# Self-attention values projected with the activations stationary and the weights moving

## The chip, the cores and the metric

The kernel runs on one core of a Trainium2 chip. The metric is the device time of one execution in microseconds. A core has TensorE (matmuls; PE in the profile, with PEld for its loading of the stationary operand), VectorE (DVE), ScalarE (ACT), GpSimd (POOL) and SyncE (SP), which here issues all the DMA transfers. Matmul results go to PSUM, and the other engines bring them to SBUF.

## The reference, cut to what matters

One inference step of a 2-layer encoder with 256 prompt tokens and 32 decode tokens, width 1024, all in fp32. Each layer has self-attention over 16 heads of 64, cross-attention into 256 memory tokens and a SwiGLU network. In layer 0, eight heads are chunked attention (A) and eight are stick-breaking attention (B); in layer 1 all sixteen are forgetting attention (C).

```python
def proj_ab(h, w_in):
    ...
    parts = jnp.split(h @ w_in, cuts, axis=-1)      # q, k, v of A; q, k, v of B

def proj_c(h, w_in, b_f):
    z = h @ w_in
    q, k, v = z[..., :w], z[..., w:2 * w], z[..., 2 * w:3 * w]     # then 16 forget gates
...
p = softmax(q @ k * 64 ** -0.5 + bias);  o = p @ v
```

`h` is the RMS-normalised input. The new keys and values of all tokens are outputs as well. The cut lines above are shortened; the reference reshapes to heads of 64 in between.

## The kernel before, in words

**Layout.** Activations are kept transposed: 8 tiles of 128 features by 288 tokens (256 prompt, then 32 decode). A projection (`project`, L151) takes a unit of weights, 128 output features by 1024 inputs, 512 KB. `unit` (L132) loads it into a staging tile `st` (four of them); ScalarE rounds it to fp32r (`hi`, five tiles, L141), VectorE takes the rest (`lo`, four tiles, L142). The activations are split likewise into `hh` and `hl` when a block of x is ready (`Next.block`, L257; `split_scaled`, L241). `mm3` (L145) makes three fp32r matmuls a block, hi by hh, hi by hl and lo by hh, with the weights stationary and 288 tokens moving: 24 matmuls for a unit. The norm's factor is not applied to h; it multiplies the result when PSUM is evacuated, since the sums of squares are ready only later (`Next.scale`, L270; `cur.then` holds evacuations back until the factor `cur.r` is there).

**Pairs of heads.** A unit is a pair of heads, so layer 0 has 24 units (`mix_ab`, L763) and layer 1 has 24 and one for the gates (`mix_c`, L870). `pairs` (L803) goes over eight pairs: project q, k and v of a pair (`evac_q` L716, `evac_kv` L721), start its attention, and insert some steps of the cross-attention's memory projections. Attentions are generators: each project calls `tick` (L176), which lets every attention that is under way make its next step, so that softmax on the other engines runs under the next projection.

**The values.** v comes out as features by tokens, and the product with the probabilities needs tokens on partitions. `v_natural` (L328) therefore transposes v on TensorE in three pieces (L330 to L332, tile `vt`) and ScalarE copies them to `vn` (L334, L335). `prompt_pv` (L380) and `sample_pv` (L407) use it as the stationary and the moving operand.

**Order.** The tile framework orders the instructions of each engine ahead of the run, by the order of the program and its own estimates; each engine then goes through its list in order. SyncE's list holds weight loads, cache and bias loads and the stores, so that a load that waits for a staging tile holds what stands behind it. At the start the first unit (`first`, L74) is loaded in three parts between the parts of x; `rel_lines` (L731) builds a skewed copy of layer 0's bias in DRAM with eight transfers (`skew`), from which every pair of A loads its bias. Layer 1 opens with `begin` (L162): six of eight blocks of two projections, which run while the last blocks of h and the norm's factor are made.

**Pools.** 74 token tiles of 128x288 (`tk`), five `vn` tiles of 384, four PSUM banks for projections (`pj`) and four for attention (`at`). `hidden` (L665) places the 44 tiles of the SwiGLU's hidden layer in `tk`, `w`, `ca` and `w2`; `room` (L584) lends `vn` and `bi` to the cross-attention.

Of the kernel before, what the change touches and what calls it, by code (L numbers as in the profile page):

```python
# [15 lines left out]
P = 128  # L16
# [10 lines left out]
def encoder_step(ctx: ExitStack, tc: tile.TileContext, a):  # L27
# [9 lines left out]
    tk = ctx.enter_context(tc.tile_pool(name="tk", bufs=74))  # L37
# [36 lines left out]
    first = wp.tile([P, 1024], F32, tag="st", bufs=4, name="first")  # L74

    def first_part(c0, c1):
        DMA.dma_start(first[:, c0:c1], a["w_ab"][0][:, c0:c1])

    first_part(0, 256)
    for i in range(4):  # L80
        DMA.dma_start(xh[i], a["xT"][:, 2 * i * NT:2 * (i + 1) * NT])
        if i == 0:
            DMA.dma_start(gain, a["gains"])
            first_part(256, 512)
        if i == 1:
            first_part(512, 1024)
# [45 lines left out]
    def unit(src, st=None, pieces=1):  # L132

        if st is None:
            st = wp.tile([P, 1024], F32, tag="st", bufs=4, name=name("st"))
            DMA.dma_start(st, src)
        hi = wp.tile([P, 1024], F32R, tag="hi", bufs=5, name=name("hi"))
        lo = wp.tile([P, 1024], F32R, tag="lo", bufs=4, name=name("lo"))
        for c in range(pieces):
            b = slice(c * 1024 // pieces, (c + 1) * 1024 // pieces)  # L140
            S.copy(hi[:, b], st[:, b])  # L141
            V.tensor_tensor(lo[:, b], st[:, b], hi[:, b].bitcast(F32), ALU.subtract)  # L142
        return hi, lo
# [107 lines left out]
    class Next:  # L251


        def __init__(self, gi):
            self.gi, self.norm, self.h, self.waiting = gi, Norm(hurry=gi == 8), ([], []), []

        def block(self, m, start=False):  # L257
            g = gain[:, self.gi * KT + m:self.gi * KT + m + 1]
            if self.gi < 8:
                hi, lo = split_scaled(x[m], g, act=True)  # L260
                self.h[0].append(hi)
                self.h[1].append(lo)
            else:
                t = tok("xg")
                V.tensor_scalar(t, x[m], g, None, op0=ALU.mult)
                self.h[0].append(t)
            if not start:
                self.norm.add(x[m])

        def scale(self):  # L270

            if self.gi != 1:
                yield 1
            y = self.norm.columns()
# [53 lines left out]
    def v_natural(v):  # L328
        p = att("vt")
        T.transpose(p[:, 0:128], v[:, 0:128], ident)  # L330
        T.transpose(p[:, 128:256], v[:, 128:256], ident)
        T.transpose(p[0:NS, 256:384], v[:, 256:288], ident)  # L332
        vn = wk.tile([P, 384], F32, tag="vn", bufs=5, name=name("vn"))
        S.copy(vn[:, 0:256], p[:, 0:256])  # L334
        S.copy(vn[0:NS, 256:384], p[0:NS, 256:384])  # L335
        return vn
# [20 lines left out]
    def attend_prompt(q, k, v, vns, j, bias, oh, ol):  # L357

        vn = vns[j] = v_natural(v)
        e = []  # L360
        for hd in range(2):
            r = slice(64 * hd, 64 * hd + 64)
            s = att("sc")
            mm(s[:, 0:128], q[r, 0:128], k[r, 0:128])
            mm(s[:, 128:384], q[r, 128:256], k[r, 0:256])
            e.append(work("e"))
            softmax(s, QT, bias[hd], e[hd])
        yield 1
        w = []
        for hd in range(2):  # L370
            t = att("tp")
            T.transpose(t[:, 0:128], e[hd][:, 0:128], ident)
            T.transpose(t[:, 128:256], e[hd][:, 128:256], ident)
            T.transpose(t[:, 256:384], e[hd][:, 256:384], ident)
            w.append(work("pt"))
            S.copy(w[hd][:, 0:384], t[:, 0:384])
        yield 1
        prompt_pv(w, vn, oh, ol)

    def prompt_pv(w, vn, oh, ol):  # L380
        po = att("po")
        for hd in range(2):
            r = slice(64 * hd, 64 * hd + 64)
            mm(po[r, 0:256], vn[:, 64 * hd:64 * hd + 64], w[hd][:, 0:256], True, False)
            mm(po[r, 128:256], vn[:, 128 + 64 * hd:192 + 64 * hd], w[hd][:, 256:384], False, True)
# [21 lines left out]
    def sample_pv(w, at, vns, cv, o):  # L407
# [8 lines left out]
        for h in range(4):  # L416
            j, hd = h // 2, h % 2
            c, n = at(j, hd)
            mm(po[32 * h:32 * h + 32, 0:64], w[0:NS, n:n + 32], vns[j][0:NS, 256 + 64 * hd:320 + 64 * hd], False, True)
# [39 lines left out]
    def stick_prompt(q, k, v, vns, j, oh, ol):  # L459
        vn = vns[j] = v_natural(v)  # L460
# [112 lines left out]
    def cross(layer, cur, memory, nxt):  # L573
# [10 lines left out]
        def room(s, i):  # L584

            if i < 10:
                return wk.tile([P, NP], F32R, tag=("vn", "bi")[i % 2], bufs=5, name=name(s))
# [77 lines left out]
    def hidden(s, i):  # L665

        if i < 26:
            return tok(s, F32R)
        i -= 26
        if i < 8:  # L670
            return wk.tile([P, NT], F32R, tag="w", name=name(s))
        if i < 12:
            return wk.tile([P, NT], F32R, tag="ca", bufs=4, name=name(s))
        if i % 2 == 0:
# [46 lines left out]
    def evac_kv(cur, p, dst):  # L721
# [41 lines left out]
    def mix_ab(cur, nxt, memory, w0):  # L763
        o = ([tok("oh", F32R) for _ in range(KT)], [tok("ol", F32R) for _ in range(KT)])
        qs, ks, vs, vns = {}, {}, {}, {}
        w = a["w_ab"]

        def proj(j):
            b = 12 * (j // 4) + j % 4
            kv = 8 * (j // 4) + j % 4  # L770
            qs[j] = evac_q(cur, project(w[b], cur.h, w=w0 if j == 0 else None))
            if j == 0:
                proj.line = rel_lines()
            ks[j] = evac_kv(cur, project(w[b + 4], cur.h), a["kv0"][kv])
            vs[j] = evac_kv(cur, project(w[b + 8], cur.h), a["kv0"][kv + 4])

        def attend(j):
            args = (qs[j], ks[j], vs[j], vns, j)
# [14 lines left out]
        pairs(proj, attend, sample, memory, (0, 0, 0, 0, 2, 2, 2, 8))  # L793
# [9 lines left out]
    def pairs(proj, attend, sample, memory, steps):  # L803
        for j in range(8):
            proj(j)
# [64 lines left out]
    def mix_c(cur, nxt, memory, w0):  # L870
# [11 lines left out]
        qs, ks, vs, vns = {}, {}, {}, {}  # L882

        def proj(j):
            qs[j] = evac_q(cur, project(w[j], cur.h, begun=begun[1] if j == 0 else None))
            ks[j] = evac_kv(cur, project(w[8 + j], cur.h), a["kv1"][j])
            vs[j] = evac_kv(cur, project(w[16 + j], cur.h), a["kv1"][8 + j])

        def attend(j):
# [13 lines left out]
            return attend_prompt(qs[j], ks[j], vs[j], vns, j, bias, o[0][j], o[1][j])  # L903
# [20 lines left out]
        pairs(proj, attend, sample, memory, (3, 1, 1, 1, 1, 1, 1, 5))  # L924
# [4 lines left out]
    w0 = None  # L929
# [27 lines left out]
    "yT": (8, 128, 288), "kv0": (16, 128, 288), "kv1": (16, 128, 288), "lf": (288, 16),  # L957
# [4 lines left out]
def _pack(inputs):  # L962
# [17 lines left out]
    def vals(c):  # L980
# [5 lines left out]
    w_c = np.pad(g["w_in_c"][0], ((0, 0), (0, 112)))  # L986
# [5 lines left out]
        "w_ab": units(g["w_in_ab"][0]), "w_oab": units(g["w_out_ab"][0]),  # L992
# [41 lines left out]
```

## Time and profile before

| | |
|---|---|
| median of 3 runs | 981.52 us (979.58 to 983.31) |
| the profiled execution | 981.77 us |
| its span | 979.9 us |
| TensorE busy, instructions | 960.9 us (98%), 7449 |
| VectorE, ScalarE, GpSimd busy | 60%, 49%, 20% |
| DMA | 163.59 MB, 167 GB/s over the span |
| mean granted clock of TensorE | 0.993 |

In the profile's rows a matmul's duration runs to its modelled end, so consecutive ones overlap; how fast they pass is seen from their starts, or from the count in a window. `128*128 128x288` is a stationary operand of 128 rows by 128 columns and a moving one of 128 partitions by 288 columns. `a<-b,c` is the tile written and the tiles read, the moving operand first. A plain fp32 matmul leaves two records, an fp32r matmul or a transpose one. In the chain of waits a line has the start, the length and what it was; in a timeline, start, length, engine, line, operation and count.

### The profile page before, as it was taken

To read this page: it belongs to the slowest core of one execution; us is meant where nothing else is said; L and a number is where in the kernel's file an instruction comes from. 1 tells how busy PE (TensorE), PEld (TensorE's weight loads), DVE (VectorE), ACT (ScalarE), POOL (GpSimd) and SP (SyncE) were. 2 spreads that over 40 slices of the span, in tenths; PEclk is the share of its full clock that TensorE was granted. 3 is DMA by queue.
4 is the path that set the end of the run, shared out by engine and by line. 5 is a ranking of instruction groups with operands and counts; after the bars stand their busy time and mean duration, and the time that the engine had idled before them with its cause. 6 is when DMAs were issued, how large, how long until landed. Compare 5 with 4: busy or idle time off the path is not lost.

```text
span 979.9 us, 19034 instructions
## 1 busy us (share of the span) xinstructions
PE 960.9 (98%) x7449; PEld 925.1 (94%) x7449; DVE 589.5 (60%) x1135; ACT 483.8 (49%) x854; POOL 194.6 (20%) x293
## 2 busy tenths in 40 slices
PE   8999999999999999999999999999999999999995
PEld 7789999998899999999998999999989999999995
DVE  6686454677676555764565666657757655555452
ACT  5556767555455444444444545445546544444330
POOL 3121001210113222411003234213002222222010
PEclk9999999999999999999999999999999999999997
DMA  7775345544254454455455555545425444444431
GB/s 235 247 248 192 127 165 174 169 168 143 91 179 158 165 173 167 178 193 173 166 201 167 179 191 182 170 160 194 149 100 168 155 159 165 173 164 166 165 109 49
DMA packets 60137, 163.59 MB, mean 167 GB/s; under 512 B 8160, under 2 KB 21520, under 8 KB 60048
## 3 DMA queue, kind: packets, MB, share of 16 engines
q1 hardware_dynamic: 60048, 162.38, 49.0%
q8 instruction: 59, 0.97, 0.4%
q14 instruction: 30, 0.25, 0.1%
HBM read 152.20 MB, written 11.72 MB: 167 GB/s over the span
## 4 chain that ended last, share of the span: by engine, by line
PE 90%; DMA 3%; DVE 3%; issue 1%; ACT 1%; SPq 0%; POOL 0%; DVEq 0%; ACTq 0%; POOLq 0%
PE pj L68 50%; PE dn L68 14%; PE op L68 11%; PE mv L68 5%; DMA st<-w_ab 2%; PE zb L68 1%; PE xs L68 1%; PE xo L68 1%; PE po L68 1%; DVE lo L142 1%; DMA skew<-lined 1%; PE sc L68 1%; PE nr L68 1%; ACT hi L141 1%; PE zs L68 1%
## 5 line engine op out<-in xcount | busy, mean ns | idle before, releaser
L141 ACT CAST hi<-st 128x1024 fp32r<-128x1024 f32 x260 | 272.2, 1049 | 339.4 <-issue 146.9
L68 PE MATMUL pj<-hh,hi 128*128 128x288 f32 (+1 forms) x1352 | 405.1, 300 | 0.0
L68 PE MATMUL pj<-hl,hi 128*128 128x288 f32 (+1 forms) x1352 | 399.8, 296 | 1.7 <-DVE hl L248 1.7
L142 DVE TENSOR_TENSOR lo<-st,hi 128x1024 fp32r<-128x1024 f32 x260 | 323.3, 1244 | 128.8 <-PE dn L68 41.3
L68 PE MATMUL pj<-hh,lo 128*128 128x288 f32 (+1 forms) x1352 | 399.4, 295 | 0.0
L68 PEld LDWEIGHTS pj<-hh,hi 128*128 128x128 f32 x1352 | 256.6, 190 | 6.2 <-issue 4.7
L68 PEld LDWEIGHTS pj<-hl,hi 128*128 128x128 f32 x1352 | 256.5, 190 | 3.3 <-DVE hl L248 3.2
L68 PEld LDWEIGHTS pj<-hh,lo 128*128 128x128 f32 x1352 | 256.7, 190 | 0.0
L68 PE MATMUL dn<-fh,hi 128*128 128x288 f32 x400 | 108.7, 295 | 0.0
L68 PE MATMUL dn<-fh,lo 128*128 128x288 f32 x352 | 103.7, 295 | 0.0
L68 PE MATMUL dn<-fl,hi 128*128 128x288 f32 x304 | 89.5, 294 | 0.0
L68 PE MATMUL op<-ol,hi 128*128 128x288 f32 x256 | 75.5, 296 | 0.0
L68 PE MATMUL op<-oh,lo 128*128 128x288 f32 x256 | 75.5, 295 | 0.0
L68 PE MATMUL op<-oh,hi 128*128 128x288 f32 x256 | 75.1, 296 | 0.0
L68 PEld LDWEIGHTS dn<-fh,hi 128*128 128x128 f32 x400 | 72.5, 188 | 0.0
L68 PEld LDWEIGHTS dn<-fh,lo 128*128 128x128 f32 x352 | 66.1, 188 | 0.0
L213 POOL TENSOR_TENSOR ssq<-ssq,sq 128x288 f32<-128x288 f32 (+1 forms) x37 | 37.0, 1000 | 120.0 <-ACT sq L202 77.8
L68 PEld LDWEIGHTS dn<-fl,hi 128*128 128x128 f32 x304 | 57.1, 188 | 0.0
L691 POOL TENSOR_TENSOR fl<-us,fh 128x288 fp32r<-128x288 f32 x38 | 32.8, 863 | 119.0 <-ACT fh L690 119.0
L686 DVE TENSOR_TENSOR us<-pj,rstd 128x288 f32<-128x288 f32 x44 | 20.1, 457 | 59.4 <-PE pj L68 59.4
L687 POOL TENSOR_TENSOR gs<-gs,sg 128x288 f32<-128x288 f32 x44 | 38.8, 882 | 75.5 <-ACT sg L685 75.5
L68 PEld LDWEIGHTS op<-ol,hi 128*128 128x128 f32 x256 | 48.2, 188 | 0.8 <-issue 0.8
(253 smaller groups left out, 1213.7 us busy)
## 6 DMA issues: line engine op xcount, KB each, us to landing
st<-w_gate SPq DMA_DIRECT2D x44, 512.0 KB, 3.3
st<-w_up SPq DMA_DIRECT2D x44, 512.0 KB, 3.2
st<-w_down SPq DMA_DIRECT2D x44, 512.0 KB, 3.3
st<-w_c SPq DMA_DIRECT2D x25, 512.0 KB, 3.3
st<-w_ab SPq DMA_DIRECT2D x23, 512.0 KB, 4.2
st<-w_xk SPq DMA_DIRECT2D x16, 512.0 KB, 3.6
st<-w_xv SPq DMA_DIRECT2D x16, 512.0 KB, 3.5
st<-w_xq SPq DMA_DIRECT2D x16, 512.0 KB, 4.3
```

The lines of the kernel that those rows point to most:

```text
L68: T.matmul(out, lhsT, rhs, start=start, stop=stop, skip_group_check=True)
L141: S.copy(hi[:, b], st[:, b])
L142: V.tensor_tensor(lo[:, b], st[:, b], hi[:, b].bitcast(F32), ALU.subtract)
L213: eng.tensor_tensor(s[:, :self.n], self.acc[i][:, :self.n], q[:, :self.n], ALU.add)
L686: V.tensor_tensor(us, pu[:, :NT], cur.r, ALU.mult)
L687: G.tensor_tensor(gs, gs, sg, ALU.mult)
L691: G.tensor_tensor(lo, us, hi.bitcast(F32), ALU.subtract)
```

## The change

All values of four pairs (512 columns of weights) are projected at once, by `project_values`, with h as the stationary operand (128 features by 128 tokens) and the weights moving (512 columns). The result has tokens on partitions, so `v_natural` is gone. A group has four units of 1024 columns, each holding two blocks of input features by 512. For the 256 prompt tokens a unit makes 2 blocks x 3 split products x 2 halves = 12 matmuls into two PSUM banks. For the 32 decode tokens it makes 2 x 4 matmuls in plain fp32, from `hs` (unsplit h of the decode tokens) and the unsplit weights in `st`, each with 32 stationary and 128 moving columns, one for each quarter of the output partitions, into a third bank. Evacuation multiplies by the norm's factor per token (a column, `cur.y`), on ScalarE for one half of the prompt and VectorE for the other and for the decode tokens.

Group 0 of layer 0 becomes the first work of the kernel, with its four units loaded between the parts of x; `rel_lines` is placed ahead of it. Group 1 comes ahead of pair 2. In layer 1 group 0 comes ahead of the gates' projection, and `begin` is no longer used there. The `k` outputs remain features by tokens; the value outputs are now tokens by features. Fewer token tiles (69), six `vn` tiles of 512, and `hidden` takes four of them. The host code that packs weights and unpacks outputs follows suit.

```diff
-    tk = ctx.enter_context(tc.tile_pool(name="tk", bufs=74))
+    tk = ctx.enter_context(tc.tile_pool(name="tk", bufs=69))
...
-    first = wp.tile([P, 1024], F32, tag="st", bufs=4, name="first")
-
-    def first_part(c0, c1):
-        DMA.dma_start(first[:, c0:c1], a["w_ab"][0][:, c0:c1])
-
-    first_part(0, 256)
+    first = [wp.tile([P, 1024], F32, tag="st", bufs=4, name=f"first{i}") for i in range(4)]
+
+    def first_part(i, c0, c1):
+        DMA.dma_start(first[i][:, c0:c1], a["w_v"][0, i][:, c0:c1])
+
+    first_part(0, 0, 512)
     for i in range(4):
         DMA.dma_start(xh[i], a["xT"][:, 2 * i * NT:2 * (i + 1) * NT])
         if i == 0:
             DMA.dma_start(gain, a["gains"])
-            first_part(256, 512)
-        if i == 1:
-            first_part(512, 1024)
+            first_part(0, 512, 1024)
+        else:
+            first_part(i, 0, 1024)
...
-        return hi, lo
+        return hi, lo, st
...
+            if gi < 2:
+                self.hs = wk.tile([P, KT * NS], F32, tag="hs", bufs=1, name=name("hs"))
...
+                if self.gi < 2:
+                    V.tensor_scalar(self.hs[:, NS * m:NS * m + NS], x[m][:, NP:NT], g, None, op0=ALU.mult)
...
-    def v_natural(v):
-        p = att("vt")
-        T.transpose(p[:, 0:128], v[:, 0:128], ident)
...
+    def project_values(src, cur, outs, vns, group, w0=None):
+
+
+        h = cur.h
+        p, p_s = [acc("vp") for _ in range(2)], acc("vps")
+        for u in range(4):
+            w = w0[u] if w0 else unit(src[u])
+            with tc.issue_after(warmed.ins):
+                for kk in range(2):
+                    k, c = 2 * u + kk, 512 * kk
+                    for part, wt in ((0, 0), (1, 0), (0, 1)):
+                        for t in range(2):
+                            mm(p[t], h[part][k][:, 128 * t:128 * t + 128], w[wt][:, c:c + 512], k == 0 and part + wt == 0,
+                               k == KT - 1 and wt == 1)
+                for kk in range(2):
+                    k, c = 2 * u + kk, 512 * kk
+                    for j in range(4):
+                        mm(p_s[32 * j:32 * j + 32, 0:128], cur.hs[:, 32 * k:32 * k + 32], w[2][:, c + 128 * j:c + 128 * j + 128],
+                           k == 0, k == KT - 1)
+            if u > 0 or group > 0:
+                tick()
+        vt = [wk.tile([P, 512], F32, tag="vn", bufs=6, name=name("vn")) for _ in range(3)]
+
+        def go():
+            y = cur.y
+            S.activation(vt[0], p[0], AF.Copy, scale=y[:, 0:1])
+            V.tensor_scalar(vt[1], p[1], y[:, 2:3], None, op0=ALU.mult)
+            for j in range(4):
+                r = slice(32 * j, 32 * j + 32)
+                V.tensor_scalar(vt[2][0:NS, 128 * j:128 * j + 128], p_s[r, 0:128], y[96:128, 4:5], None, op0=ALU.mult)
+            for t in range(2):
+                DMA.dma_start(outs[0][group, t], vt[t])
+            DMA.dma_start(outs[1][group], vt[2][0:NS])
+
+        cur.then(go)
...
-            mm(po[r, 0:256], vn[:, 64 * hd:64 * hd + 64], w[hd][:, 0:256], True, False)
+            mm(po[r, 0:256], vn[0][:, 64 * hd:64 * hd + 64], w[hd][:, 0:256], True, False)
...
-        if i < 26:
+        if i < 22:
             return tok(s, F32R)
...
         active.append(cur.scale())
-        pairs(proj, attend, sample, memory, (0, 0, 0, 0, 2, 2, 2, 8))
+        proj.line = rel_lines()
+        values(0)
+        pairs(values, proj, attend, sample, memory, (0, 0, 0, 1, 2, 2, 2, 7))
...
-    def pairs(proj, attend, sample, memory, steps):
+    def pairs(values, proj, attend, sample, memory, steps):
         for j in range(8):
+            if j == 2:
+                values(1)
             proj(j)
...
-        begun = begin([w[24], w[0]], cur.h)
...
         active.append(cur.scale())
-        p = project(w[24], cur.h, begun=begun[0])
+        values(0)
+        p = project(w[16], cur.h)
...
         cur.block(m, start=True)
-        if m == 1:
-            w0 = unit(None, first, 4)
+        if m % 2 == 1:
+            w0.append(unit(None, first[m // 2], 2))
```

More of the change, by code (lines that the diff above doesn't have):

```diff
@@ L273, in scale @@
                 yield 1
-            y = self.norm.columns()
+            y = self.y = self.norm.columns()
             yield 1
@@ L326, in split_o @@
         V.tensor_tensor(ol, p, oh.bitcast(F32), ALU.subtract)
-    def v_natural(v):
-        p = att("vt")
[L330 to L336, printed above, removed]
+    def project_values(src, cur, outs, vns, group, w0=None):
[29 more added lines that the diff above has]
+        cur.then(go)
+        for j in range(4):
+            vns[4 * group + j] = [t[:, 128 * j:128 * j + 128] for t in vt]
     def softmax(s, cols, bias, out):
@@ L991, in _pack @@
         "gains": gains.reshape(9, 8, 128).transpose(2, 0, 1).reshape(128, 72),
[L992 removed]
+        "w_ab": units(w_ab[:, :, 0:2].reshape(1024, 2048)),
+        "w_v": w_v.reshape(4, 4, 2, 128, 512).transpose(0, 1, 3, 2, 4).reshape(4, 4, 128, 1024),
+        "w_oab": units(g["w_out_ab"][0]),
         "w_c": units(w_c), "w_oc": units(g["w_out_c"][0]),
```

68 lines of the change are left out of this document (37 added, 31 removed), and 2 rows, old and new, of the table _OUTS.

## The prediction

> **What bounds the kernel now.** I read the page first, then busy time by stage, then the timeline of TensorE and the chain of waits where the change lies.
>
> ```profile
> span 979.9 us, 19034 instructions
> PE 960.9 (98%) x7449; PEld 925.1 (94%) x7449; DVE 589.5 (60%) x1135; ACT 483.8 (49%) x854; POOL 194.6 (20%) x293
> PE 90%; DMA 3%; DVE 3%; issue 1%; ACT 1%; SPq 0%; POOL 0%; DVEq 0%; ACTq 0%; POOLq 0%
> ```
>
> TensorE carries 90% of the chain that ended last. Busy time says little about its pace, since the records overlap; counts in the windows do. Columns: length, then busy time and number of instructions of each engine, granted clock, DMA share, GB/s.
>
> ```profile
> core 0: us, PE busy (x) PEld busy (x) DVE busy (x) ACT busy (x) POOL busy (x), PEclk, DMA share, GB/s
> ...
> 27.19:60.00 32.81, 30.60 (x255) 26.63 (x254) 23.01 (x71) 17.72 (x46) 4.91 (x15) 1.00 0.76 245
> 60.00:177.50 117.50, 116.93 (x959) 108.73 (x959) 68.39 (x139) 80.53 (x142) 13.28 (x15) 1.00 0.53 174
> ...
> 293.00:422.86 129.86, 129.86 (x987) 129.86 (x986) 81.17 (x121) 61.21 (x86) 41.12 (x43) 1.00 0.49 169
> ...
> 503.00:531.00 28.00, 25.51 (x186) 23.43 (x185) 16.47 (x44) 15.63 (x29) 5.18 (x11) 0.94 0.48 163
> ```
>
> From 293 to 423 us almost all of the 987 matmuls have 288 columns: 129.86/987 = 0.1316 us each, a stream without holes. So in steady state a microsecond comes off the kernel only if TensorE issues a microsecond less. There are holes at two places: the first 60 us, where the DMA share is 0.76, and 503 to 531 us (186 instructions in 28 us).
>
> **What leaves TensorE, per group of four pairs.** Each pair loses its value projection, 24 x 0.1316 = 3.16 us, and three transposes:
>
> ```profile
> 523.47 0.29 PE L68 MATMUL pj<-hh,lo 128*128 128x288 f32 x1
> 523.60 0.27 PE L330 MATMUL vt<-ident,kv 128*128 128x128 f32 x1
> 523.71 0.27 PE L331 MATMUL vt<-ident,kv 128*128 128x128 f32 x1
> 523.82 0.27 PE L332 MATMUL vt<-ident,kv 128*32 128x128 f32 x1
> 524.02 0.93 PE L68 MATMUL sc<-kv,q 64*128 64x128 f32 x8
> ...
> 36.91 0.29 PE L68 MATMUL pj<-hl,hi 128*128 128x288 f32 x1
> 37.04 0.29 PE L68 MATMUL pj<-hh,lo 128*128 128x288 f32 x1
> 37.27 0.88 PE L68 MATMUL po<-pt,vn 128*64 128x256 f32 x8
> ```
>
> The transposes take 524.02-523.60 = 0.42 us. But going from full-array matmuls to matmuls on part of the array costs extra: 37.27-37.04 = 0.23 against 0.13, 0.10 us more. The third transpose bears that now, and the projection before the scores will bear it then, so 0.32 us leaves. Per group: 4 x (3.16+0.32) = 13.9 us.
>
> **What comes: 48 matmuls with 512 moving columns.** No row has 512. The widest of this type has 384:
>
> ```profile
> 97.42 0.34 PE L68 MATMUL zb<-sh,ntrir 128*128 128x384 f32 x1
> 97.60 0.34 PE L68 MATMUL zb<-sl,ntrir 128*128 128x384 f32 x1
> 97.78 0.38 PE L68 MATMUL zb<-ab,nones 128*128 128x128 f32 x2
> ...
> 16.56 0.44 PE L68 MATMUL pj<-hh,hi 128*128 128x288 f32 x1
> 16.80 0.44 PE L68 MATMUL pj<-hl,hi 128*128 128x288 f32 x1
> 17.04 0.37 PE L68 MATMUL pj<-hh,lo 128*128 128x288 f32 x1
> 17.25 0.29 PE L68 MATMUL pj<-hh,hi 128*128 128x288 f32 x1
> 17.38 0.29 PE L68 MATMUL pj<-hl,hi 128*128 128x288 f32 x1
> ```
>
> 384 columns: (97.78-97.42)/2 = 0.18 us, 0.469 ns a column; 288: 0.457 ns. Upper end 0.240 us for 512. Lower end: before 17.04 us matmuls of 288 start 0.24 us apart, 0.833 ns a column; were the later pace exactly twice that, 512 would take 0.213. I take 0.234 (0.457 ns a column, which the 384 confirms): 48 x 0.234 = 11.2 us, between 10.2 and 11.5.
>
> Here a rule disagrees with the row. The Trainium skill, "TensorE: Matmul & The Clock Gate", section "Back-to-back issue gap", gives N/2.4 + 2.5 ns for a warm isolated matmul: 216 ns at 512, and 122.5 ns at 288, where the trace has 131.6. By the rule the 48 would be an estimated 10.4 us. I go by the rows; the rule's outcome is a rival.
>
> **And 32 narrow matmuls for the 32 decode tokens**, plain fp32, 32 columns of the array by 128 moving, each four on the four strips of the array. The nearest rows are the sample scores (four strips, 128 moving, half the rows) and the sample's value product (four strips, 64 moving, all rows); each matmul gives two records.
>
> ```profile
> 42.64 0.44 PE L68 MATMUL ss<-ca,q 64*32 64x128 f32 x8
> 42.88 0.26 PE L68 MATMUL ss<-kv,q 64*32 64x32 f32 x8
> ...
> 53.16 0.32 PE L68 MATMUL os<-ca,pts 128*32 128x64 f32 x8
> 53.41 0.31 PE L68 MATMUL os<-vn,pts 32*32 32x64 f32 x8
> 53.65 0.40 PE L68 MATMUL pj<-hh,hi 128*128 128x288 f32 x1
> ```
>
> Eight records of 128 columns pass in 0.24 us, where a single 128-column transpose takes 0.11: four run side by side, in two turns of 0.12. The full-row case does the same (eight of 64 in 0.25, the switch included). A weight unit has eight such matmuls, so four turns, 0.48 us, and a switch of about 0.10 in and out: 0.68. Per group 4 x 0.68 = 2.7 us. Were the strips to run one after another: 16 x 0.12 + 0.2 = 2.1 per unit, 8.5 per group.
>
> **Sum on TensorE:** 11.2 + 2.7 = 13.9 against 13.9. The wide matmul gains 12.6-11.2 = 1.4 us over the old projections, the dropped transposes 1.3, and the decode tokens eat both. Per group 0 (from -1.0 to +0.3 with the strips parallel), over four groups 0 (-4 to +1).
>
> **Other engines.** One row each:
>
> ```profile
> L142 DVE TENSOR_TENSOR lo<-st,hi 128x1024 fp32r<-128x1024 f32 x260 | 323.3, 1244 | 128.8 <-PE dn L68 41.3
> ...
> L334 ACT COPY vn<-vt 128x256 f32<-128x256 f32 x16 | 5.9, 367 | 0.1
> L335 ACT COPY vn<-vt 32x128 f32<-32x128 f32 x16 | 4.0, 250 | 0.0
> L725 DVE TENSOR_TENSOR kv<-pj,rstd 128x288 f32<-128x288 f32 x32 | 14.3, 450 | 15.7 <-PE pj L68 15.7
> ```
>
> The weight splits stay, 4 a group. ScalarE loses 4 x 0.62 us a group and gains one 512-wide evacuation; VectorE trades 4 x 0.45 for one 512-wide and four small ones, and gets eight small products for the decode tokens per layer. VectorE at 60% and ScalarE at 49% lie under TensorE's stream; were the cover gone it would be about 2 us a group. Four stores a group become three. Nothing on the path.
>
> **Staging.** The narrow matmuls read the unsplit weights, so a value unit's staging tile comes free when TensorE ends the unit, not when VectorE has made lo. Look-ahead falls to three units of 11.2/4 + 0.68 = 3.5 us, 10.4 us. A refill takes 5.0 us landing at its slowest in the start (row below), 1.05 for hi (the ACT hi row there), 1.24 for lo: 7.3. It fits unless SyncE's queue, where stores, bias and cache loads stand behind the waiting weight load, holds it over 3 us. Cost 0 to 2 us a group; I take 0 and count the first group below.
>
> Token tiles fall from 74 to 69. A norm square already waited on one; later blocks of the next norm in the output projection will wait for attention outputs to be read, inside the last 3.2 us pass. 0 to 3 us; I take 0.
>
> **The start.** Here the order changes most: 13.9 us of matmuls on four units come first, fed two x blocks and one weight unit at a time.
>
> ```profile
> 0.00:5.00 5.00, 3.43 (x32) 3.33 (x32) 0.42 (x1) 2.37 (x5) 3.57 (x23) 1.00 0.48 135
> 5.00:10.00 5.00, 4.38 (x14) 3.10 (x13) 4.41 (x6) 3.49 (x10) 4.08 (x7) 1.00 0.97 340
> ...
> 5.11:27.19 22.08, 18.85 (x96) 16.85 (x96) 1.19 (x3) 1.00 0.80 262
> ...
> 11.59 0.61 PE L68 MATMUL pj<-hl,hi 128*128 128x288 f32 x1 [1.09 <-DVE hl L248]
> ...
> 15.55 7.39 DMA skew<-lined
> ...
> 23.37 5.00 DMA st<-w_ab
> 28.45 1.06 ACT hi L141
> ```
>
> Bytes: 0.67 MB by 5 us, then 0.34 MB/us. The four unit-and-x steps need 0.84, 1.66, 2.48, 3.30 MB: 5.5, 7.9, 10.3, 12.8 us. The first matmul comes 0.13 MB later than at 5.11, so 5.6. From there each pair of splits feeds six wide matmuls, not three narrow ones, so I expect no wait like the 1.09 us before 11.59. In the old trace the slow pace ends at 17.04, 5.4 us after matmuls run unbroken (the granted clock reads 1.00 on both sides, the spacing shows it); so in the new one near 11.0. A slow unit lasts 12 x 0.427 + 1.1 = 6.2 us, a fast one 3.5: the first ends at 11.5, the others at 15.0, 18.5, 22.0; with the norm's matmuls (18.83 to 20.09, and 0.6) about 23.9. Then q of pair 0: 27.1.
>
> Old at 27.19: 96 projection matmuls, four projections, 12.6 us of work. New at 27.1: 13.9 + 3.2 = 17.1 us. Lead 4.4 us. With the slow pace to 17.04 as before it is 1.3.
>
> Does it last? From 27.19 to 60 us 255 instructions ran where the next stage's rate (959/117.5) gives 268: 1.6 us of holes, and the chain of waits there runs through the eight skew transfers and weight loads behind them. The skew now lies under the value matmuls, which helps; but the same loads are wanted 4 us sooner. I give back 1.5 (0 to 4.4). Start: -2.9 (-4.4 to +0).
>
> **Layer 1's entry.** The opening of two projections on six of eight blocks goes; the value units cover the norm instead (36 matmuls before block 6 is needed). The gate's chain to the first bias keeps its cover of one projection and three memory steps. 0, bounds -3 to +2.
>
> **Sum.** The profiled execution took 981.77 us (span 979.9 and 1.9 around it). 981.77 + 0 - 2.9 = 978.9; the median of the runs is 0.25 lower, so 978.6.
>
> **Rivals.**
> 1. *512 columns stream at 0.213 us.* Speaks for it: at 17.04 us the pace nearly doubles, and 0.213 is the exact double. Against: 288 and 384 both lie 10% or more above it. 48 x 0.021 x 4 = 4.0 us: 974.6. The Trainium skill's rule quoted above would give nearly the same.
> 2. *The lead is eaten.* The first 60 us wait on transfers, so TensorE arrives sooner and waits longer, on staging tiles held by the narrow matmuls or behind skew in SyncE's queue. Against: 3.3 MB are now asked for in one unbroken run. 981.5, no change.
> 3. *Slower: the strips don't run side by side with 128 rows and 128 columns.* Two at a time: eight turns, 1.16 a unit, +1.9 a group, +7.7: 986.3, and 989.2 without the lead. One at a time: +5.8 a group, +23: 1002. It decides from about 0.9 us a unit, where it cancels the lead. For it: no row has all 128 rows with 128 columns. Against: both neighbours overlap fourfold.
>
> **How the numbers follow.** I call 0.5%, 4.9 us, what a measurement can tell from no change, so faster is below 976.6 and slower above 986.4. Forecast 978.6: 0.52, of which 0.13 falls below 976.6 (lead kept whole, fewer holes). Rival 1: 0.16. Rival 2: 0.20. Rival 3: 0.12, all but 0.02 above 986.4; with unknown stalls taken from rival 2, slower 0.13. Faster 0.29, same 0.58. The range 972.5 to 985 holds rivals 1 and 2 with the bounds of start and tiles, and leaves out rival 3.
>
> **What would show it.** The new wide matmuls 0.234 us apart (0.213: rival 1); eight narrow ones of a unit in about 0.68 us, switches included (over 0.9: rival 3); the slow pace ending near 11 us; the first query projection beginning near 24 us; the stage up to 60 us with no more holes than now. The forecast is wrong if TensorE's count of instructions per microsecond drops in the attention stages, or if weight loads enter the chain in them.

## The result and the profile after

The changed kernel takes 990.73 us (median of 5 runs, 987.13 to 992.12) against 981.52 us before: a ratio of 1.0089, with a 95% interval of 1.0064 to 1.0113. It is 9.2 us slower, where 978.6 was forecast and 985 was the upper end. The profiled execution took 992.12 us, the longest of the five; the one of before took 981.77. What the profiles show below is therefore a loss of 10.4 us, about a microsecond more than the medians.

The page of the profile after: the span, the engines' busy time, the shares of the chain that ended last.

```profile
span 990.4 us, 19040 instructions
...
PE 964.0 (97%) x7465; PEld 913.4 (92%) x7465; DVE 598.7 (60%) x1156; ACT 480.2 (48%) x827; POOL 196.2 (20%) x293
...
PE 87%; DMA 5%; DVE 4%; issue 2%; ACT 1%; POOL 1%; SPq 0%; DVEq 0%; POOLq 0%; ACTq 0%
```

TensorE has 16 more instructions and VectorE is 9 us busier, but none is near its limit except TensorE, and TensorE's share of the chain falls from 90% to 87%, and DMA's rises from 3% to 5%. So something is waited for. Three places in the timeline of TensorE cut the kernel into stages: the first matmul of layer 0's output projection (`op`), the first of layer 1, and the first of layer 1's output projection. Before:

```profile
177.34 0.30 PE L68 MATMUL op<-oh,hi 128*128 128x288 f32 x1
...
492.56 0.29 PE L68 MATMUL pj<-hh,hi 128*128 128x288 f32 x1
...
650.80 0.30 PE L68 MATMUL op<-oh,hi 128*128 128x288 f32 x1
```

and after:

```profile
181.26 0.29 PE L68 MATMUL op<-oh,hi 128*128 128x288 f32 x1
...
496.38 0.39 PE L68 MATMUL vp<-hi,hh 128*128 128x512 f32 x1
...
661.88 0.30 PE L68 MATMUL op<-oh,hi 128*128 128x288 f32 x1
```

| stage | before | after | difference |
|---|---|---|---|
| start and layer 0's self-attention | 177.34 | 181.26 | +3.9 |
| rest of layer 0 | 315.22 | 315.12 | -0.1 |
| layer 1's self-attention | 158.24 | 165.50 | +7.3 |
| from there to the span's end | 329.1 | 328.5 | -0.6 |

The loss lies in the two stages that the change touches. The windows of after show what it is made of (columns as in the prediction: length; busy time and instructions of PE, PEld, DVE, ACT, POOL; granted clock; DMA share; GB/s):

```profile
27.00:60.00 33.00, 30.10 (x210) 25.26 (x208) 16.44 (x49) 14.08 (x33) 2.39 (x16) 0.90 0.68 220
...
531.00:565.00 34.00, 30.28 (x209) 25.84 (x208) 17.64 (x49) 14.17 (x33) 14.05 (x33) 0.87 0.28 87
...
28.20:31.60 3.40, 3.40 (x16) 3.40 (x16) 0.59 (x2) 0.00 (x0) 0.00 (x0) 0.52 1.02 298
...
35.10:38.50 3.40, 3.40 (x15) 3.40 (x16) 0.39 (x1) 1.16 (x2) 0.14 (x1) 0.53 0.63 231
...
530.00:536.80 6.80, 6.80 (x34) 6.06 (x32) 2.81 (x6) 1.57 (x3) 0.74 (x1) 0.51 0.37 107
...
560.70:564.10 3.40, 3.40 (x10) 2.72 (x11) 1.90 (x3) 1.06 (x2) 2.86 (x6) 0.52 0.00 0
```

and of before, where the same windows read as follows, with the only stretch at half clock that it has ahead of the last 12 us, in which TensorE has next to nothing to do:

```profile
27.00:60.00 33.00, 30.79 (x256) 26.82 (x255) 23.01 (x71) 17.72 (x46) 4.91 (x15) 1.00 0.76 245
...
531.00:565.00 34.00, 34.00 (x294) 31.28 (x293) 21.46 (x58) 17.02 (x42) 12.56 (x29) 1.00 0.54 179
...
515.50:518.90 3.40, 3.40 (x18) 3.40 (x18) 2.04 (x4) 1.76 (x3) 0.73 (x2) 0.51 0.15 47
```

In the first of these windows 210 matmuls run where 256 did, in the second 209 where 294 did (a wide matmul counts as one and lasts longer, so the counts exaggerate). The granted clock, 1.00 before, has a mean of 0.90 and 0.87. After some of the holes TensorE goes on at about half its clock, for 3.4 or 6.8 us.

The holes themselves stand in TensorE's timeline, where the bracket has the idle time and what ended it. After:

```profile
26.54 0.85 PE L68 MATMUL nr<-ident,y 128*128 128x128 f32 x6 [2.34 <-DVE y L230]
...
33.80 0.40 PE L68 MATMUL pj<-hh,hi 128*128 128x288 f32 x1 [1.62 <-ACT hi L141]
...
35.06 0.61 PE L68 MATMUL pj<-hh,lo 128*128 128x288 f32 x1 [0.73 <-DVE lo L142]
...
529.40 1.08 PE L68 MATMUL gc<-tri,lf 128*16 128x256 f32 x4 [2.88 <-DVE lf L879]
...
547.19 0.30 PE L403 MATMUL tp<-ident,e 128*128 128x128 f32 x1 [1.18 <-DVE e L385]
...
560.67 0.47 PE L430 MATMUL ts<-ident,es 128*128 128x128 f32 x1 [1.92 <-DVE es L385]
```

Before, holes at corresponding places were:

```profile
32.65 0.30 PE L372 MATMUL tp<-ident,e 128*128 128x128 f32 x1 [0.73 <-DVE e L353]
...
513.40 0.82 PE L68 MATMUL gc<-tri,lf 128*16 128x256 f32 x4 [1.11 <-DVE lf L843]
...
529.56 0.30 PE L372 MATMUL tp<-ident,e 128*128 128x128 f32 x1 [1.22 <-DVE e L353]
```

The start has more holes than are shown. Counted from 0.6 us on, those of before up to layer 0's output projection make 4.5 us (beside the 0.73 shown, 1.57 us ahead of the first matmul, 1.09 at 11.59 and 1.09 at 48.33), and those of after 8.6 (beside the three shown, the same 1.57, 0.77 at 5.94, 0.82 at 61.17 and 0.75 at 96.86). These two kinds of loss account for the table within a microsecond. In the start the holes grow by 4.1 us, and 6.8 us at half clock cost about another 3.4: +7.5, against a forecast of -2.9 that became +3.9, a difference of 6.8. In layer 1 the holes grow from 2.3 to 6.0 us and the half-clock stretches from 3.4 to 10.2, which is worth about 3.4: +7.1, against +7.3.

**Why the holes are there, at the start.** SyncE's timeline of after, with `st` the staging tiles:

```profile
18.36 0.30 SPq L771 DMA_DIRECT2D lined<-line  x1
18.76 0.33 SPq L136 DMA_DIRECT2D st<-w_ab  x1
...
25.38 0.34 SPq L136 DMA_DIRECT2D st<-w_ab  x1
```

The last of the first four units has been asked for by 6.07 us. From then to 18.76 no weight of the self-attention is asked for. Before, two went out at 4.99, the line's store at 12.26, and two more behind it at 12.60:

```profile
4.99 0.82 SPq L136 DMA_DIRECT2D st<-w_ab  x2
12.26 0.30 SPq L738 DMA_DIRECT2D lined<-line  x1
```

The waits of SyncE's queue in the whole of the profile after name two reasons (total, times, longest):

```profile
SPq L136 <- PE vps L68: 20.3, 7, 8.0
...
SPq L771 <- DVE line L769: 4.9, 1, 4.9
```

Before, a staging tile came free with `lo`; now seven loads wait for the narrow matmuls (`vps`) to read theirs, up to 8.0 us. The second is the store of the bias line: its copy on VectorE is now behind all the splits of the four value units. The first weight after the values, q of pair 0, is thus split when the norm wants VectorE:

```profile
23.18 1.22 DVE L142 TENSOR_TENSOR lo<-st,hi 128x1024 fp32r<-128x1024 f32 x1 [3.36 <-ACT hi L141]
24.32 0.16 DVE L225 TENSOR_SCALAR ms<-nrm 128x6 f32<-128x6 f32 x1
```

The norm's chain (L225 to L230) stands behind `lo` in VectorE's list, `lo` waits 3.36 us for `hi`, and `hi` for the load asked for at 18.76. TensorE waits 2.34 us for `y`, and then 1.62 for the next load, asked for at 25.38 behind the eight skew transfers. The chain of waits that ends in these holes goes from the line's copy (18.20, 0.14 us) through its store (18.36, 1.38 us) and the skew transfers (19.75, 5.56 us) to this load (start, length):

```profile
25.38 7.24 DMA st<-w_ab
```

**In layer 1** the same pattern stands on ScalarE. After and before, the gates' chain:

```profile
519.81 0.24 ACT L869 ACTIVATE gate_e<-gate_z 128x48 f32<-128x48 f32 x1
521.54 1.05 ACT L141 CAST hi<-st 128x1024 fp32r<-128x1024 f32 x1 [1.49 <-DMA st<-w_c]
522.61 1.28 ACT L870 ACT_TABLE_LOAD   x1
```

```profile
506.40 0.24 ACT L833 ACTIVATE gate_e<-gate_z 128x48 f32<-128x48 f32 x1 [2.09 <-DVE gate_z L831]
506.67 1.28 ACT L834 ACT_TABLE_LOAD   x1
```

Before, 0.27 us pass between the two; after, 2.80, because a `hi` that waits for its load stands in between.

### The profile page after: what moved, and what is told of

It is laid out like the page before. It is cut to its first block, busy times and chain, and to the rows that moved or that the text cites. A ratio compares the mean times of both kernels' runs of the same rounds, so it can differ in the third digit from the quotient of the medians.

```text
span 990.4 us, 19040 instructions
## 1 busy us (share of the span) xinstructions
PE 964.0 (97%) x7465; PEld 913.4 (92%) x7465; DVE 598.7 (60%) x1156; ACT 480.2 (48%) x827; POOL 196.2 (20%) x293
## 4 chain that ended last, share of the span: by engine, by line
PE 87%; DMA 5%; DVE 4%; issue 2%; ACT 1%; POOL 1%; SPq 0%; DVEq 0%; POOLq 0%; ACTq 0%
PE pj L68 45%; PE dn L68 14%; PE op L68 10%; PE mv L68 5%; PE vp L68 2%; PE zb L68 1%; DVE lo L142 1%; PE xs L68 1%; PE xo L68 1%; DMA st<-w_ab 1%; PE po L68 1%; DMA st<-w_xk 1%; PE sc L68 1%; DMA st<-w_c 1%; ACT hi L141 1%
## 5 line engine op out<-in xcount | busy, mean ns | idle before, releaser
L68 PE MATMUL pj<-hh,hi 128*128 128x288 f32 (+1 forms) x1224 | 365.5, 299 | 1.6 <-ACT hi L141 1.6
L68 PE MATMUL pj<-hh,lo 128*128 128x288 f32 (+1 forms) x1224 | 361.4, 295 | 0.7 <-DVE lo L142 0.7
L68 PE MATMUL pj<-hl,hi 128*128 128x288 f32 (+1 forms) x1224 | 360.6, 295 | 0.0
L68 PEld LDWEIGHTS pj<-hh,hi 128*128 128x128 f32 x1224 | 232.2, 190 | 6.7 <-issue 4.0
L68 PEld LDWEIGHTS pj<-hh,lo 128*128 128x128 f32 x1224 | 232.4, 190 | 1.4 <-DVE lo L142 1.0
L68 PEld LDWEIGHTS pj<-hl,hi 128*128 128x128 f32 x1224 | 232.6, 190 | 0.0
L213 POOL TENSOR_TENSOR ssq<-ssq,sq 128x288 f32<-128x288 f32 (+1 forms) x37 | 33.5, 906 | 128.6 <-ACT sq L202 106.5
```

The source lines that it names most:

```text
L68: T.matmul(out, lhsT, rhs, start=start, stop=stop, skip_group_check=True)
L213: eng.tensor_tensor(s[:, :self.n], self.acc[i][:, :self.n], q[:, :self.n], ALU.add)
```

## The experiments

Four theories, called by letter where an expectation uses letters. **A**: staging tiles are held until TensorE has read them (the narrow matmuls read the raw weights), so loads go out late. **S**: the bias line's copy, late on VectorE, holds SyncE's queue at the start. **B**: layer 1 is slower because the gates' projection now comes behind the value units. **C**: layer 1's bias loses the cover that each pair's value projection gave it. Each time below is compared with runs of the kernel before on the same chip, and its ratio is to those: 981.53 us for e1, e2, e4 and e5, 982.15 for f1, f2, f4 and e8, 981.77 for f5, g1, g2 and g3. Savings are told from the changed kernel's 990.73 us, which was measured beside 981.52.

**Release of the tiles (e1_release).** The narrow matmuls read `hi`, the rounded weights, and the tile is free as soon as `lo` is made. This kernel leaves out the low part of the weights in the decode tokens' values.

```diff
-    mm(p_s[...], cur.hs[...], w[2][:, c + 128 * j:c + 128 * j + 128], ...)
+    mm(p_s[...], cur.hs[...], w[0][:, c + 128 * j:c + 128 * j + 128].bitcast(F32), ...)
```

> The narrow matmuls for the decode tokens read hi instead of the unsplit weights, so a value unit's staging tile comes free when VectorE has made lo, as for every other unit; number and shape of matmuls stay. (The decode tokens' values leave out the lo part of the weights.) Theory A, held staging tiles: in layer 1 the loads behind the value units come earlier, ScalarE no longer stands in front of a late weight load ahead of the gate's exponential, and the 3.2 us hole before the gate's sums with its half-clock stretch goes; of the 7.3 us that layer 1's self-attention lost, at least 5 come back: about 985. At the start little, since the bias store still holds SyncE's queue to 18 us. Theory B, lost cover (the gate's chain has too little TensorE work over it now, whatever the loads do): the hole stays within 1 us, total within 1.5 us of 990.7.

Measured: 979.32 us (977.6 to 982.07), ratio 0.998 (0.9967 to 0.9992). That is 11.4 us less than the changed kernel, twice what A had said, and B did not expect it at all. SyncE's timeline in this kernel:

```profile
8.60 7.21 SPq L136 DMA_DIRECT2D st<-w_ab  x3
18.31 0.30 SPq L771 DMA_DIRECT2D lined<-line  x1
```

and its window from 27 to 60 us:

```profile
27.00:60.00 33.00, 33.00 (x291) 27.65 (x292) 21.75 (x62) 14.29 (x35) 4.81 (x18) 1.00 0.83 260
```

The line's store is as late as ever, 18.31 us, but three weight loads are now ahead of it, and the window has 291 matmuls at full clock. Layer 0's output projection begins at 171.93 us, 5.4 earlier than before the change. Layer 1's self-attention takes 160.8 us, still 2.5 over before.

**The line's copy on GpSimd (e2_line).**

```diff
-        V.tensor_copy(ln[:, 0:128], ln[:, 128:129].to_broadcast([8, 128]))
+        G.tensor_copy(ln[:, 0:128], ln[:, 128:129].to_broadcast([8, 128]))
```

> The small copy that widens the bias line runs on GpSimd instead of VectorE, where it stood behind all the splits of the start. Theory S, queue order at the start: the store of the line leaves near 11 us, not 18.4; the loads of pair 0's query and key weights and the skew transfers behind it start 6 us earlier, the stalls of 2.6, 1.9 and 1.0 us between 24 and 36 us and two half-clock stretches go: 4 to 6 us, about 985.5. Rival, held staging tiles alone: the second weight load has to wait for TensorE's second value unit (15.5 us) anyway and then stands behind skew; less than 1.5 us.

Measured: 982.97 us (980.46 to 986.27), ratio 1.002 (1.0008 to 1.0032): 7.8 us less than the changed kernel, where S had expected 4 to 6. The line's store leaves at 13.45 us, and the two weight loads behind it at 14.23 and 21.03 (18.76 and 25.38 without this edit). So S alone gives back most of the loss, too.

**A fifth staging tile (e4_st5)**, paid with four token tiles.

```diff
-    tk = ctx.enter_context(tc.tile_pool(name="tk", bufs=69))
+    tk = ctx.enter_context(tc.tile_pool(name="tk", bufs=65))
...
-            st = wp.tile([P, 1024], F32, tag="st", bufs=4, name=name("st"))
+            st = wp.tile([P, 1024], F32, tag="st", bufs=5, name=name("st"))
```

> Five staging tiles instead of four, paid with four token tiles (69 to 65). Theory A: one more unit of look-ahead, so part of what the release gives, 2 to 5 us: about 987. Theory B: nothing. If token tiles are what is short, slower than 990.7 by 1 us or more, with longer waits of ScalarE's squares in the output projections.

Measured: 983.2 us (980.67 to 987.7), ratio 1.0017 (1.0002 to 1.0032): 7.5 us less, more than the 2 to 5 that A had expected. One weight load now goes out ahead of the line's store, at 6.80 us. A held tile can be replaced by another, and token tiles are not what is short.

**Gates first in layer 1 (e5_gate).** The gates' projection opens the layer through `begin`, as before, and the value units follow.

```diff
+        begun = begin([w[16]], cur.h)
+        p = project(w[16], cur.h, begun=begun[0])
+        cur.then(lambda: start(gate(cur, p, cum, lf, bf)))
         values(0)
-        p = project(w[16], cur.h)
-        cur.then(lambda: start(gate(cur, p, cum, lf, bf)))
```

> Layer 1 opens with the gate's projection (six blocks early, as in the kernel before) and the value units come behind it, so the gate's chain runs under 13.9 us of value matmuls. Theory B, lost cover: the 3.2 us hole before the gate's sums and the half clock after it (6.8 us) go, and the first bias is ready in time: 5 to 7 us, about 984.5. Theory A: the hole moves to the next load that is late; less than 2.5 us.

Measured: 986.13 us (983.06 to 987.69, 4 runs), ratio 1.0056 (1.0039 to 1.0073): 4.6 us less, between the two. In the profiled execution, the fastest of the four, the hole before the gates' sums is 0.46 us, and layer 1's self-attention takes 158.6 us, 6.9 less than in the changed kernel, as much as B had expected of the whole.

The savings, 11.4, 7.8, 7.5 and 4.6, add up to 31 where the loss is 9.2. So they are not separate causes. The following runs separate them.

**Narrow matmuls first (f1_narrow_first).** In each unit the eight narrow matmuls go ahead of the twelve wide ones, so that the tile is free about 2.8 us sooner.

```diff
                 for kk in range(2):
                     k, c = 2 * u + kk, 512 * kk
+                    for j in range(4):
+                        mm(p_s[...], cur.hs[...], w[2][...], k == 0, k == KT - 1)
+                for kk in range(2):
+                    k, c = 2 * u + kk, 512 * kk
                     for part, wt in ((0, 0), (1, 0), (0, 1)):
...
-                for kk in range(2):
-                    k, c = 2 * u + kk, 512 * kk
-                    for j in range(4):
-                        mm(p_s[...], cur.hs[...], w[2][...], k == 0, k == KT - 1)
```

> The whole computation; only the order within a value unit changes: the eight narrow matmuls that read the staging tile come ahead of the twelve wide ones, so the tile comes free about 2.8 us earlier in each unit, and no instruction is added or taken away. Theory A, held staging tiles: most of the 11.4 us that the early release gave, 6 to 10 us: about 982.5. Rival, the release helped because hi was read instead of the raw tile (another buffer, another order of TensorE), not because of when staging came free: less than 2 us, about 990.

Measured: 983.14 us (980.39 to 986.42), ratio 1.0014 (1.0 to 1.0028). Reading the same tile a little sooner is worth as much as a fifth tile. One weight load goes out ahead of the line's store, at 9.15 us. This bears out A by another edit, and the rival that it names, with less than 2 us, has fallen.

**Release in one layer at a time (g1_release_l0, g2_release_l1)**: the edit of the first experiment where `cur.gi` is 0, or 1.

> The release of the staging tiles in layer 0 alone (there the narrow matmuls read the rounded weights, which leaves out the low part of the weights in the decode tokens' values of layer 0; layer 1 as in the changed kernel). Released in both layers the time fell from 990.7 to 979.3 us, and in the profiles 9.5 us of the gain stood at the start of layer 0's output projection (181.4 to 171.9) and 3 to 5 us in layer 1. If the two places add up: about 982.5 us. If the start alone mattered: 979.3. If any change of SyncE's list gives back the same slack wherever it is made: 983, and the layer 1 release gives the same.

> The release in layer 1 alone. If the two places add up: about 986.5 to 987.5 us, with the output projection of layer 0 beginning at 181 us as in the changed kernel and layer 1 shorter by 3 to 5 us. If the start alone mattered: 990.7. If any change gives back the same slack: 983.

Measured: 986.9 us (984.07 to 989.22, 4 runs) and 986.09 us (985.31 to 988.32, 4 runs), ratios 1.0054 (1.0037 to 1.0071) and 1.0041 (1.0026 to 1.0057). Windows of the first and then of the second:

```profile
27.00:60.00 33.00, 33.00 (x291) 27.50 (x284) 21.19 (x61) 14.02 (x35) 4.81 (x18) 1.00 0.79 254
...
531.00:565.00 34.00, 30.07 (x240) 23.22 (x239) 17.52 (x49) 14.03 (x35) 13.29 (x31) 0.95 0.29 100
```

```profile
27.00:60.00 33.00, 28.37 (x208) 23.61 (x208) 16.48 (x49) 14.18 (x33) 2.04 (x14) 0.95 0.67 218
...
531.00:565.00 34.00, 30.38 (x259) 24.04 (x259) 19.67 (x50) 16.18 (x36) 13.32 (x32) 1.00 0.48 154
```

Each release mends its own layer: 291 matmuls in the early window with the first and 208 with the second; clocks the other way round in the late one. In the profiled executions the first stage is 8.4 us shorter with the first (172.89 against 181.26) and layer 1's self-attention 6.7 us shorter with the second (158.8 against 165.5). By the medians the gains are 3.8 and 4.6 us, 8.5 of 11.4; layer 0's is less than expected. The stages say more than the medians, since the fastest of four executions stands there beside the slowest of five. That the start alone mattered has fallen, and so has the view that any change of SyncE's list gives back the same slack, by which both would be at 983. With executions of one kernel 3 to 5 us apart and four runs each, the remaining 3 us stay open.

**The hold without the change (g3_before_st3).** The kernel before, with three staging tiles.

```diff
-            st = wp.tile([P, 1024], F32, tag="st", bufs=4, name=name("st"))
+            st = wp.tile([P, 1024], F32, tag="st", bufs=3, name=name("st"))
```

> The kernel before, without the change, with three staging tiles in place of four: a loss of look-ahead of one unit, by itself. The prediction's step says that three units of 3.16 us, 9.5 us, still cover a refill of 7.3 us: by it the time stays within 1 us of 981.5. The theory that look-ahead is what the changed kernel lost says that SyncE's in-order list holds loads longer than the 2.2 us left: 985 to 992 us, with idle time of TensorE in the first 60 us and at layer 1's entry.

Measured: 986.01 us (984.46 to 986.66, 6 runs), ratio 1.0037 (1.0025 to 1.0049): 4.2 us slower than with four. In TensorE's timeline and in the window:

```profile
28.95 0.40 PE L68 MATMUL pj<-hh,hi 128*128 128x288 f32 x1 [0.96 <-ACT hi L141]
```

```profile
27.00:60.00 33.00, 28.49 (x225) 25.00 (x224) 21.08 (x59) 15.81 (x39) 4.22 (x15) 0.95 0.70 223
```

Without any value units, one unit less of look-ahead makes a hole of the same kind on `hi` in the same window (225 matmuls for 256), with 0.73 us on `lo` behind it. The clock falls less than in the changed kernel, to a mean of 0.95, and it does so after a later hole, 1.77 us on `e`, ended at 50.43. The first stage is 3.1 us longer than before (180.44 us), layer 1's self-attention is not (158.2). The sum of a refill (7.3 us) against three units (9.5 us) had allowed the three tiles.

**Bias ahead (f2_release_bias).** Release in both layers, and layer 1's bias of pairs 1 to 7 loaded and built ahead of the pair's q and k projections.

```diff
+            if j > 0:
+                ahead[j] = make_bias(j)
...
-        def attend(j):
+        def make_bias(j):
...
+            return bias
+        def attend(j):
+            bias = ahead.pop(j) if j in ahead else make_bias(j)
```

> As with the early release, and in layer 1 the load and the building of a pair's bias come ahead of its query and key projections (pairs 1 to 7), not behind them. (The decode tokens' values leave out the lo part of the weights.) Theory C, lost cover: without the value projection between a pair's keys and its scores the bias comes too late; the holes of 0.6, 0.7, 0.5 and 2.3 us at 544 to 548 us and the half clock behind them go, 3 to 6 us below the early release: about 975. Rival, VectorE is the limit there (softmax of two heads and of the sample within one value unit): the holes stay, within 1.5 us of 979.3.

Measured: 976.53 us (973.42 to 980.99), ratio 0.9945 (0.9931 to 0.996), and 2.8 us less than the release alone. The release alone has, in the timelines of VectorE and TensorE,

```profile
546.22 0.33 DVE L380 CUSTOM_DVE_ANT_0 es<-ss,bcs 128x160 f32<-128x160 f32 x1 [0.93 <-POOL bcs L958]
...
548.16 0.33 PE L430 MATMUL ts<-ident,es 128*128 128x128 f32 x1 [1.90 <-DVE es L385]
```

VectorE waits there for a bias (`bcs`) that GpSimd has built late, behind the pair's bias, and TensorE waits for VectorE. The load for the pair's bias, `ck`, goes out at 535.38 us and the pair's scores begin at 538.66, 3.3 us later; in the kernel before it goes out at 531.23 and they begin at 538.21, 7.0 us later, with the value projection between. With the bias ahead this hole is gone: layer 1's self-attention takes 157.9 us, 0.3 less than before the change. C holds. The half clock that C had expected to go with it has only moved: another hole, 1.39 us ended at 535.63, is followed by 3.5 us at 0.52, and the mean clock from 531 to 565 us is 0.95 with the bias ahead and without it.

**Release, line and gates together (e8_all).**

> Early release, the bias line's copy on GpSimd and the gate's projection ahead of the value units. (The decode tokens' values leave out the lo part of the weights.) If the line's wait at the start is a cost of its own, the early release's remaining start stalls go as well (2.4 us before the second half of the norm's sums and a half-clock stretch, about 3 us), and the gate's hole of 1.1 us: about 975. If the line and the gate only mattered because the loads were late already, it stays within 1.5 us of 979.3.

Measured: 980.06 us (978.05 to 982.77), ratio 0.998 (0.9967 to 0.9993): no better than the release alone. This fits S and B being places at which a late load did harm, not causes beside it: with the tiles released, the two edits together are worth nothing.

**The edits put together (f5_nf_bias_line, f4_all).** Both have the narrow matmuls first, the bias ahead and the line on GpSimd; the second opens layer 1 with the gates as well.

> The whole computation, narrow matmuls first in each unit, layer 1's bias built a pair ahead, the line's copy on GpSimd, and layer 1 opened by the value units as in the changed kernel (without the gate first). With the gate first as well it took 975.4 us. If late loads were all that made the place of the gate matter: 975 to 977. If the gate's place has a worth of its own: 978 to 980.

> The whole computation, with narrow matmuls first, the bias ahead, the line's copy on GpSimd and the gate's projection first. If each of the causes stands, it lies below the kernel before by more than the early release did: about 974, between 970 and 979. If narrow first doesn't release staging early enough, about 980.

Measured: 977.88 us (976.95 to 979.28, 4 runs), ratio 0.9955 (0.994 to 0.997), and 975.4 us (974.85 to 978.26, 4 runs), ratio 0.9928 (0.9912 to 0.9945). Both are faster than the kernel before and the changed one. Whether the gates' place is worth anything here stays open: the intervals overlap.

## Why the prediction was wrong, point by point

**The wide matmuls: right.** TensorE's timeline after:

```profile
9.82 1.05 PE L68 MATMUL vp<-hi,hl 128*128 128x512 f32 x2
10.67 0.79 PE L68 MATMUL vp<-lo,hh 128*128 128x512 f32 x2
...
11.96 0.72 PE L68 MATMUL vp<-hi,hh 128*128 128x512 f32 x2
...
13.93 0.62 PE L68 MATMUL vp<-hi,hl 128*128 128x512 f32 x2
14.39 0.62 PE L68 MATMUL vp<-lo,hh 128*128 128x512 f32 x2
14.94 0.64 PE L68 MATMUL vps<-first,hs 128*32 128x128 f32 x16
15.52 0.74 PE L68 MATMUL vp<-hi,hh 128*128 128x512 f32 x2
```

Two start every 0.46 us, 0.23 each, as taken from the 288 and 384 columns (0.234). Rival 1 with 0.213 is out, and so is the outcome of the Trainium skill's formula ("TensorE: Matmul & The Clock Gate", section "Back-to-back issue gap"), 216 ns.

**The narrow matmuls: right.** The unit from 11.96 to 15.52 lasts 3.56 us; 11.2/4 + 0.68 = 3.48 was forecast. Sixteen records pass in 0.58 us, so the strips do run side by side. Rival 3, the one that was slower, is out: the kernel is slower by another way.

**The start: right until 24 us.** The slow pace ends at about 11 us, as forecast (the two from 9.82 take 0.85, those from 13.93 take 0.46), and the four units and the norm's matmuls end at 26.54 - 2.34 = 24.2, where 23.9 was expected. But the 2.34 us for `y` follow, and the query projection begins only after the factor's transposes (`nr`, from 26.54), not at 24.

**Staging: the step that failed.** "It fits unless SyncE's queue ... holds it over 3 us. Cost 0 to 2 us a group; I take 0". The first unit's tile was free at 11.96 us and the second's at 15.52, where the next units' wide matmuls begin. The loads into the next tiles went out at 18.76 and 25.38: 6.8 and 9.9 us late. The refill too was longer than reckoned: the second load landed in 7.24 us, with `hi` and `lo` 9.5, where 7.3 was taken. But even that is under 10.4; the fault is that the comparison was made of durations alone, and the wait in SyncE's list was named and put at nothing. A load goes out when its tile is free and everything ahead of it in SyncE's list has gone too, and in this list, ordered ahead of the run by the framework's own estimates, a tile that comes free later puts its load later: with the tiles released three loads go out from 8.60, with the narrow matmuls first or a fifth tile one, and in the changed kernel none before the line's store. The hold cost 11.4 us, more than the upper bound of 8 for four groups, as several of the holes brought half a clock with them, and late loads held ScalarE's and VectorE's lists. That one unit of look-ahead is worth several us is seen in the old kernel as well (+4.2 with three tiles).

**The lead: underrated.** Once tiles were released, layer 0 came out 5.4 us ahead in the profiled execution, where -2.9 with a bound of -4.4 was forecast. The whole change, so released, is 2.2 us faster than before: close to the forecast of 2.9, though made up of a larger lead and a loss in layer 1.

**Layer 1's entry: wrong.** "The gate's chain to the first bias keeps its cover" was to be 0, between -3 and +2. It was +7.3. Of this the hold had the larger part: the stage takes 165.5 us in the changed kernel, 160.8 with the release in both layers and 158.8 with the release in layer 1 alone. The rest, 0.6 to 2.5 us in these executions and 2.8 by the medians with and without the bias ahead, is the cover of each pair's v projection, under which the bias of that pair was loaded and built. The 0.6 and the 2.5 both have the hole of 1.90 us on `es`, once without half clock behind it and once with. I had counted what those 3.16 us did for TensorE, and not what lay beneath them.

**Other engines and token tiles.** Their busy time is indeed nothing, and 65 token tiles instead of 69 did no harm together with a fifth staging tile. What was overlooked is their order: a `lo` or `hi` that waits for a load holds the norm's chain or the gates' behind it.

**Rival 2 named the place and mispriced it.** "TensorE arrives sooner and waits longer, on staging tiles held by the narrow matmuls or behind skew in SyncE's queue": that is what happened, but its price was capped at the lead, so that it ended at no change. Nothing caps a wait at the lead.

## What to carry to other kernels

Where a new reader takes hold of a staging tile, count when its load can go out, with all that stands ahead of it in the issuing queue, and not only whether a refill fits under the compute; a test with one tile less prices this before anything is rebuilt. Where matmuls are moved from each step to one block, list what lay under them at the old place. And if several fixes each give back most of a loss, run them together before calling any of them a second cause.

## What was not expected of the hardware

Idle times of 2.34 us (ended at 26.54) and 2.88 us (ended at 529.40) were followed by stretches of 3.4 and 6.8 us at a granted clock of 0.52 and 0.51. The last hole, 1.92 us, came with a stretch from 560.7 on, and the 1.11 us at 513.40 in the kernel before was followed by one as well. The 1.18 us at 547.19 was not, nor the 1.22 us at 529.56 in the kernel before. One and the same hole went both ways: the 1.90 us on `es` were followed by 3 us at 0.50 in the run with the release (ended at 548.16), and by a clock of 1.00 in the run with the release in layer 1 alone (ended at 555.72). So the length of a hole alone does not decide it. About half of such a stretch is lost, so a hole followed by one cost about 1.7 or 3.4 us beside its own length. The Trainium skill, "TensorE: Matmul & The Clock Gate", section "HAM oscillation — how this bites in real kernels", asks for no idle gaps over about 3.4 us; here half clock followed shorter ones, and the measurement decides. Which of the shorter ones it follows is not settled by these runs.
